# Turning blocks on all partitions at once, and copying them to their place, in a two-layer hybrid encoder

## The chip, the cores and the metric

The kernel runs on one core of a Trainium2 chip. The core has five engines, each with its own in-order stream of instructions: TensorE (PE in the profile) multiplies matrices, VectorE (DVE), ScalarE (ACT) and GpSimd (POOL) work elementwise, and SyncE (SP) here only issues transfers. The metric is the device time of one execution in microseconds (us), as the median over several runs. A profile is one further execution, recorded by the hardware.

## The reference

The input is one sequence of 256 positions with 2048 channels, in float32. There are two layers. Each layer is a token mixer with a residual, and then a gated MLP with a residual; a final normalisation follows.

```python
for i in range(DEPTH):                        # DEPTH = 2
    hn = rms_norm(h, mix_norm[i])
    h = h + (mixer_a if i % 2 == 0 else mixer_b)(hn, ...)
    h = h + conv_ffn(rms_norm(h, ffn_norm[i]), w_up[i], conv_w[i], conv_b[i], w_down[i])
return rms_norm(h, final_norm)

def conv_ffn(h, w_up, conv_w, conv_b, w_down):   # D_FF = 5632
    u = depthwise_conv3(h @ w_up) + conv_b       # along the positions
    gate, val = jnp.split(u, 2, axis=-1)
    return (jax.nn.silu(gate) * val) @ w_down
```

Mixer A (layer 0) is grouped-query attention: 16 query heads and 4 key/value heads of 128 channels, queries and keys normalised per head and rotated by their position. Mixer B (layer 1) has 24 heads of 128 channels in three groups of eight; the groups look at nearby positions at strides 1, 4 and 16, with a relative-position bias, and are weighted against each other by their softmax denominators. Both end in an output projection back to 2048 channels.

## The kernel before, in words

**Layout.** The 256 positions are held as 2 x 128: position 2p + m lies on partition p in half m. The residual stream `h` is a tile [128, 2, 2048]. A matrix product needs its left operand with channels on the partitions, so before each projection the activations have to be transposed: 16 tiles `xh` of 128 channels by 256 positions, called hT in the code.

**Projections.** Every product is computed to nearly full float32 precision from a high and a low half. `feed` (line 137) loads weights in pieces of 128 x 1024 on SP's queue into six raw buffers. `split_raw` (line 125) makes the halves: ScalarE copies the piece to the reduced type (`wh`, line 128), VectorE subtracts it from the original (`wl`, line 129). Three such pairs of buffers rotate. For each piece TensorE then runs 12 matmuls of 512 columns (lines 153 to 155: high x high, high x low, low x high, for two channel blocks and two halves of the positions). Such a piece with its 12 matmuls is called a unit here. `project` makes 512 output columns from eight units or more; `project2` makes two column blocks, holding back the part of the left operand that is ready last; `project_pair` (line 278 among its matmuls) does two column blocks of the MLP's down projection with one multiplication fewer per 2 x 2 block.

**Side work in steps.** Everything else, such as attention, the MLP's convolution and the transposes, is written as Python generators. `start` puts one in a list; after each unit, `step` (line 93) runs the first generator up to its next `yield`. So the number of yields says how many units later a piece of work is put into the program. The framework then orders each engine's instructions by its own estimate of when they are ready; the weight halves get a priority that lies 45 instructions ahead (`AHEAD`). At run time each engine works strictly through its own stream.

**Two ways to transpose without TensorE.** VectorE's transpose turns blocks of 32 x 32. To turn a whole tile, each block must also move from one group of 32 partitions to another.

- `block_T` (line 332, the instruction is on line 334) does both in one: it reads 32 partitions and writes 32 other ones. One call covers 32 x 256 elements, so 16 calls turn a tile [128, 2, 512].
- The MLP's convolution (`up_post`, lines 428 to 449) does it in two: two transposes of 128 x 512 turn the blocks where they lie (line 435), and then 16 copies of 32 x 256 put them on their partitions (lines 444, 446, 448). The string `PLACE = "pava"` says which engine copies to each of the four groups: GpSimd four of the 16, ScalarE eight, VectorE four.

`block_T` is used in two generators. `late_transpose` (line 337) turns 512 columns of `h` just after the residual was added, for the next projection, and is called for column blocks 0 to 2 at the end of both mixers (`out_proj`, line 661) and of the first MLP; block 3 goes over TensorE. Its last part, `put`, multiplies by the gain on ScalarE (line 294) and takes the low half on VectorE (line 297). `heads_T_dve` (line 699) turns four heads of keys or queries: mixer A's keys once, mixer B's keys and queries twelve times. In mixer B's groups 1 and 2 the result is used as it is (the low half is None); otherwise it is split into two halves (lines 290, 291). Mixer A's queries go over TensorE (`heads_T`).

**Order around it.** `add_residual` (line 388, VectorE) and `sumsq_cols` (line 329, two squares on ScalarE) run when a column block is done, then `late_transpose` follows over six steps: one to allocate its tile, four of four small transposes each, and one for the gains. In `project2` of mixer A the column blocks 0 and 1 are done two units apart, and blocks 2 and 3 eight units after one another, so that three transposes follow closely. Biases for mixer B are loaded on GpSimd's queue (line 928).

Of the kernel before, what the change touches and what calls it, by code (L numbers as in the profile page):

```python
# [13 lines left out]
P = 128  # L14
D = 2048
NT = 256
# [17 lines left out]
def tile_encoder(ctx: ExitStack, tc: tile.TileContext, x, xT, w_a, w_ao, q_gain, k_gain, w_b, w_bo,  # L34
# [294 lines left out]
            nc.scalar.activation(junk(), h[:, m, n * 512:(n + 1) * 512], AF.Square,  # L329
                                 accum_out=ss[:, m, n:n + 1])  # L330

    def block_T(o, s, b, g):
        rows, cols = slice(32 * g, 32 * g + 32), slice(32 * b, 32 * b + 32)
        nc.vector.transpose(o[cols].rearrange("p a (m t) -> p a m t", m=2)[:, :, :, rows],  # L334
                            s[rows].rearrange("p m (a c) -> p a m c", c=P)[:, :, :, cols])

    def late_transpose(hT, n, g, pool, tag):
        def put(kt, src):
            hT[kt] = new_hT(kt)
            split_scaled(*hT[kt][:2], src, gain[:, g, kt:kt + 1])  # L340

        yield
        if n < 3:
            t = pool.tile([P, 4, NT], F32, tag=tag, name=nm("tT"))
            for b in range(4):
                yield
                for gr in range(4):
                    block_T(t, h[:, :, n * 512:(n + 1) * 512], b, gr)
            yield
            for j in range(4):  # L350
                put(4 * n + j, t[:, j, :])
            return
        yield
        for kp in range(2):
            if kp:
                yield
            t = ps_tile()
            for j in range(2):
                kt = 4 * n + 2 * kp + j
                for m in range(2):  # L360
                    nc.tensor.transpose(t[:, j * NT + m * P:j * NT + (m + 1) * P],
                                        h[:, m, kt * P:(kt + 1) * P], ident)
            for j in range(2):
                put(4 * n + 2 * kp + j, t[:, j * NT:(j + 1) * NT])
# [31 lines left out]
    def ffn(l, hT, ss_in, g_next, last, side=None):  # L396
        with tc.tile_pool(name=nm("wpool"), bufs=1) as wp, tc.tile_pool(name=nm("fpool"), bufs=1) as fp:
# [29 lines left out]
            def up_post(acc, n, cs, after=None):  # L427
                u = us.pop(0)
                us.append(u)
                yield  # L430
                s = fp.tile([P, 2, 512], F32, tag="s", name=nm("s"))
                t = fp.tile([P, 2, 512], F32, tag="t", name=nm("t"))
                for m in range(2):
                    nc.scalar.activation(s[:, m], acc[m], AF.Copy, scale=rstd[:, m:m + 1])
                    nc.vector.transpose(t[:, m], s[:, m])  # L435
                yield
                tv = t.rearrange("p m (j q c) -> p j m q c", j=4, q=4)
                uv = u.rearrange("p j (m t) -> p j m t", m=2)
                for i in range(16):
                    a, b = i // 4, (i // 4 + i) % 4  # L440
                    dst = uv[32 * b:32 * b + 32, :, :, 32 * a:32 * a + 32]
                    src = tv[32 * a:32 * a + 32, :, :, b]
                    if PLACE[b] == "p":
                        nc.gpsimd.tensor_copy(dst, src)  # L444
                    elif PLACE[b] == "a":
                        nc.scalar.activation(dst, src, AF.Copy)  # L446
                    else:
                        nc.vector.tensor_copy(dst, src)
# [61 lines left out]
            for hf, (p0, p1) in enumerate(HALVES):  # L510
# [39 lines left out]
                def done(accs, n):  # L550
                    if hf == 1 and last:
                        for m in range(2):
                            cols = slice(n * 512, (n + 1) * 512)
                            hs = h[:, m, cols]
                            nc.vector.tensor_tensor(hs, accs[m], hs, ALU.add)
                            if n < 3:
                                nc.scalar.activation(junk(), hs, AF.Square, accum_out=ss[:, m, n:n + 1])
                                nc.gpsimd.tensor_tensor(hs, hs, fin[n], ALU.mult)
                            else:
                                nc.vector.scalar_tensor_tensor(junk(), hs, 1.0, hs, ALU.mult, ALU.mult,  # L560
                                                               accum_out=ss[:, m, n:n + 1])
                                finish(m)
                        if n == 2:
                            nc.vector.tensor_reduce(part, ss[:, :, :3], axis=AX.X, op=ALU.add)
                            nc.vector.tensor_scalar(part, part, 1.0 / D, EPS, op0=ALU.mult, op1=ALU.add)
                        return
                    add_residual(accs, n)
                    if hf == 1:
                        sumsq_cols(ss, n, junk)
                        start(late_transpose(hTn, n, g_next, fp, "tT"))  # L570

                def finish(m):
                    ms = small.tile([P, 1], F32, tag="ms", name=nm("ms"))
# [84 lines left out]
            assert not spare  # L658
        return hTn, ss

    def out_proj(w, slots, kgs, late, g_next, junk, pool, tag):
        hTn, ss = {}, new_ss()

        def done(accs, n):
            add_residual(accs, n)
            sumsq_cols(ss, n, junk)
            start(late_transpose(hTn, n, g_next, pool, tag))

        done(project2(w, 0, 1, slots, kgs, late, lambda a: done(a, 0)), 1)
        for n in (2, 3):  # L670
# [27 lines left out]

    def heads_T_dve(o, s, pool, tag):
        hi, lo = o  # L700
        t = hi if lo is None else pool.tile([P, 4, NT], F32, tag=tag, name=nm("tT"))
        for b in range(4):
            if b:
                yield
            for g in range(4):
                block_T(t, s, b, g)
        if lo is not None:
            split(hi, lo, t)

    def mixer_a():  # L710
        with tc.tile_pool(name="apool", bufs=1) as ap:
# [165 lines left out]

            for g in range(4):
                start(attend(g, project(w_a, g, hT, kgs)))
            return out_proj(w_ao, slots, kgs, 1, 1, junk, ap, "sq")  # L880

    scr0 = dpool.tile([8, P, 512], F32, name="scr0")
    scr1 = dpool.tile([16, P, 256], F32, name="scr1")
# [26 lines left out]
    def mixer_b(hT, ss_in):  # L910
        with tc.tile_pool(name="bpool", bufs=1) as bp:
# [26 lines left out]
            for hf in range(2):  # L938
# [102 lines left out]
            return out_proj(w_bo, slots, [0, 2, 4, 1, 3, 5], 3, 3, junk, bp, "vl")  # L1041

    hT, ss = mixer_a()
    hT, ss = ffn(0, hT, ss, 2, False, bias_lines)
# [86 lines left out]
```

## Time and profile before

| | |
|---|---|
| median of 3 runs | 2273.33 us (2270.11 to 2275.6) |
| the profiled execution | 2272.74 us |
| its span, first to last instruction | 2270.9 us |
| granted TensorE clock | 0.999 |
| DMA, mean over the span | 193 GB/s |

A line of the groups view names the line of the kernel, the engine, the operation, the tile written and those read, the shape and the count; then the busy time in us and the mean ns of one; then the engine's idle time just before these instructions and what ended most of it. A line of the timeline has the start and the duration in us, the engine, the line, the operation and the tiles, and in square brackets idle time just before it. A line of the list of waits has who waited, for whom, then the sum in us, the number of times and the longest. Matmuls overlap, and their ends are modelled.

### The profile page before, as it was taken

The page shows a single profiled execution, that of the slowest core. Times are in us where ns is not written, and L with a number is a line of the kernel's source. Part 1 is how long each engine was busy: PE and PEld are TensorE (multiplying, and loading weights), DVE is VectorE, ACT ScalarE, POOL GpSimd, SP SyncE. Part 2 cuts the span into 40 slices and gives each one's busy share as a digit, 9 for nine tenths or more (in the row PEclk, how much of TensorE's full clock was granted, in tenths as well). Part 3 has the DMA queues.
Part 4 walks back from the last instruction along what each step waited for, and adds up shares of the span by engine and source line. Part 5 has one row for each costly group of instructions (what it writes and reads, how often), then busy time and mean ns, then how long its engine had stood idle before and what let it go on. Part 6 is the DMA issues. An engine that isn't in the chain of part 4 may idle for free.

```text
span 2270.9 us, 28787 instructions
## 1 busy us (share of the span) xinstructions
PE 2251.8 (99%) x10169; PEld 1861.3 (82%) x10169; DVE 1758.8 (77%) x2521; ACT 1394.8 (61%) x2066; POOL 197.2 (9%) x284
## 2 busy tenths in 40 slices
PE   9999999999999999999999999999999999999998
PEld 7788788888888888888888888878888888888886
DVE  6877877878877778978876876586888788687784
ACT  6565477677547777545454454455777754577763
POOL 2210002210001010010000000000101100001110
PEclk9999999999999999999999999999999999999999
DMA  8444557755665665666555554555665656656653
GB/s 296 158 149 148 190 193 225 222 188 190 210 204 188 198 188 186 211 215 203 190 177 176 177 193 160 179 185 195 196 193 194 205 180 218 189 192 195 223 197 128
DMA packets 126449, 437.42 MB, mean 193 GB/s; under 512 B 17264, under 2 KB 18032, under 8 KB 126304
## 3 DMA queue, kind: packets, MB, share of 16 engines
q1 hardware_dynamic: 119744, 425.64, 57.2%
q0 software_dynamic: 6128, 9.38, 1.6%
q8 instruction: 79, 1.29, 0.2%
q10 hardware_dynamic: 432, 0.56, 0.1%
q14 instruction: 66, 0.54, 0.1%
HBM read 429.20 MB, written 6.29 MB: 192 GB/s over the span
## 4 chain that ended last, share of the span: by engine, by line
PE 81%; DVE 1%; DMA 1%; issue 0%; POOL 0%; ACT 0%; POOLq 0%; DVEq 0%; ACTq 0%
PE acc L154 21%; PE acc L153 21%; PE acc L155 21%; PE acc L273 5%; PE acc L275 5%; PE acc L278 5%; DMA scr<-lnt 1%; PE ps L305 1%; DVE wl L129 1%; PE ps L1009 0%; DVE tT L334 0%; PE ps L308 0%; PE ps L309 0%; PE ps L307 0%; DVE h L388 0%
## 5 line engine op out<-in xcount | busy, mean ns | idle before, releaser
L129 DVE TENSOR_TENSOR wl<-raw,wh 128x1024 fp32r<-128x1024 f32 x822 | 1007.1, 1229 | 354.9 <-ACT wh L128 350.2
L128 ACT ACTIVATE wh<-raw 128x1024 fp32r<-128x1024 f32 x822 | 867.0, 1058 | 622.0 <-PE acc L155 394.9
L153 PE MATMUL acc<-wh,xh 128*128 128x512 f32 x2176 | 852.0, 392 | 0.8 <-ACT wh L164 0.8
L154 PE MATMUL acc<-wl,xh 128*128 128x512 f32 x2176 | 848.6, 390 | 3.6 <-DVE wl L129 2.9
L155 PE MATMUL acc<-wh,xh 128*128 128x512 f32 x2176 | 847.6, 390 | 0.0
L154 PEld LDWEIGHTS acc<-wl,xh 128*128 128x128 f32 x2176 | 408.8, 188 | 89.9 <-DVE wl L129 6.4
L155 PEld LDWEIGHTS acc<-wh,xh 128*128 128x128 f32 x2176 | 408.5, 188 | 85.0
L153 PEld LDWEIGHTS acc<-wh,xh 128*128 128x128 f32 x2176 | 408.7, 188 | 84.8 <-ACT wh L164 1.6
L273 PE MATMUL acc<-wh,ah 128*128 128x512 f32 x524 | 204.1, 390 | 0.6 <-DVE h L388 0.6
L275 PE MATMUL acc<-wh,al 128*128 128x512 f32 x524 | 203.9, 389 | 0.0
L444 POOL COPY u<-t 32x256 f32<-32x256 f32 x176 | 110.7, 629 | 1039.9 <-DVE t L435 1031.7
L154 PE MATMUL acc<-wl,ah 128*128 128x512 f32 x480 | 187.9, 392 | 2.0 <-DVE wl L129 1.8
L153 PE MATMUL acc<-wh,ah 128*128 128x512 f32 x480 | 187.4, 390 | 0.0
L155 PE MATMUL acc<-wh,al 128*128 128x512 f32 x480 | 187.1, 390 | 0.0
L446 ACT ACTIVATE u<-t 32x256 f32<-32x256 f32 x352 | 147.8, 420 | 12.6 <-DVE t L435 4.6
L278 PE MATMUL acc<-wl,ah 128*128 128x512 f32 x524 | 146.0, 389 | 0.0
L273 PEld LDWEIGHTS acc<-wh,ah 128*128 128x128 f32 x524 | 98.4, 188 | 21.7 <-DVE h L388 1.3
L278 PEld LDWEIGHTS acc<-wl,ah 128*128 128x128 f32 x524 | 98.4, 188 | 20.5
L275 PEld LDWEIGHTS acc<-wh,al 128*128 128x128 f32 x524 | 98.3, 188 | 20.3
L154 PEld LDWEIGHTS acc<-wl,ah 128*128 128x128 f32 x480 | 90.1, 188 | 24.1 <-DVE wl L129 5.8
L155 PEld LDWEIGHTS acc<-wh,al 128*128 128x128 f32 x480 | 90.1, 188 | 18.4
L153 PEld LDWEIGHTS acc<-wh,ah 128*128 128x128 f32 x480 | 90.2, 188 | 18.3
(170 smaller groups left out, 1597.9 us busy)
## 6 DMA issues: line engine op xcount, KB each, us to landing
raw<-in_w_up_dram SPq DMA_DIRECT2D x352, 512.0 KB, 4.3
raw<-in_w_down_dram SPq DMA_DIRECT2D x176, 512.0 KB, 4.7
raw<-in_w_b_dram SPq DMA_DIRECT2D x144, 512.0 KB, 3.9
raw<-in_w_bo_dram SPq DMA_DIRECT2D x48, 512.0 KB, 3.9
raw<-in_w_a_dram SPq DMA_DIRECT2D x40, 512.0 KB, 4.4
raw<-in_w_ao_dram SPq DMA_DIRECT2D x32, 512.0 KB, 3.8
raw<-in_w_a_dram SPq DMA_DIRECT2D x16, 256.0 KB, 7.2
h<-in_x_dram SPq DMA_DIRECT2D x4, 512.0 KB, 7.6
```

The costliest lines, as they stand in the source:

```text
L128: nc.scalar.activation(wh, r, AF.Copy)
L129: nc.vector.tensor_tensor(wl, r, wh.bitcast(F32), ALU.subtract)
L153: nc.tensor.matmul(accs[m], xh, wh[:, j, :], start=st, stop=False)
L154: nc.tensor.matmul(accs[m], xh, wl[:, j, :], start=False, stop=False)
L155: nc.tensor.matmul(accs[m], xl, wh[:, j, :], start=False, stop=sp)
L273: nc.tensor.matmul(acc[k], xh, wh[:, j, :], start=k in fresh, stop=False)
L275: nc.tensor.matmul(acc[k], xl, wh[:, j, :], start=False, stop=False)
L278: nc.tensor.matmul(acc[k], xh, wl[:, j, :], start=False, stop=last[k] == i and j == 1)
L305: nc.tensor.matmul(o, lh[ls], rh[rs], start=start, stop=stop)
L444: nc.gpsimd.tensor_copy(dst, src)
L446: nc.scalar.activation(dst, src, AF.Copy)
```

## The change

Both generators now take the MLP's way. What stood in `up_post` becomes two helpers, `turn_blocks` and `place_blocks`, and `turned` joins them, with one `yield` between. Its string is `"paaa"`: four of the 16 copies go to GpSimd, twelve to ScalarE, none to VectorE. The MLP itself keeps `"pava"`.

`late_transpose` needs two tiles now, one for the turned blocks and one for the result, so it is given two tags; they name buffers that the pools already have (`sq` and `t2` in mixer A, `t` and `tT` in the MLP, `vl` and `kTh` in mixer B). Its gains are spread over two steps, two tiles each; the number of steps stays six. `heads_T_dve` writes the result straight into the target where there is no low half, and otherwise back over the staging tile, from which it is split; the number of steps stays the same here too.

```diff
-    def block_T(o, s, b, g):
-        rows, cols = slice(32 * g, 32 * g + 32), slice(32 * b, 32 * b + 32)
-        nc.vector.transpose(o[cols].rearrange("p a (m t) -> p a m t", m=2)[:, :, :, rows],
-                            s[rows].rearrange("p m (a c) -> p a m c", c=P)[:, :, :, cols])
+    def turn_blocks(s, pool, tag):
+        t = pool.tile([P, 2, 512], F32, tag=tag, name=nm("tT"))
+        for m in range(2):
+            nc.vector.transpose(t[:, m], s[:, m])
+        return t
+
+    def place_blocks(o, t, place):
+        tv = t.rearrange("p m (j q c) -> p j m q c", j=4, q=4)
+        for i in range(16):
+            a, b = i // 4, (i // 4 + i) % 4
+            dst = o[32 * b:32 * b + 32, :, :, 32 * a:32 * a + 32]
+            src = tv[32 * a:32 * a + 32, :, :, b]
+            if place[b] == "p":
+                nc.gpsimd.tensor_copy(dst, src)
+            elif place[b] == "a":
+                nc.scalar.activation(dst, src, AF.Copy)
+            else:
+                nc.vector.tensor_copy(dst, src)
+
+    def turned(o, s, pool, tag):
+        t = turn_blocks(s, pool, tag)
+        yield
+        place_blocks(o.rearrange("p j (m t) -> p j m t", m=2), t, "paaa")
...
         if n < 3:
-            t = pool.tile([P, 4, NT], F32, tag=tag, name=nm("tT"))
-            for b in range(4):
-                yield
-                for gr in range(4):
-                    block_T(t, h[:, :, n * 512:(n + 1) * 512], b, gr)
+            yield
+            o = pool.tile([P, 4, NT], F32, tag=tags[1], name=nm("tM"))
+            yield from turned(o, h[:, :, n * 512:(n + 1) * 512], pool, tags[0])
+            yield
             yield
             for j in range(4):
-                put(4 * n + j, t[:, j, :])
+                if j == 2:
+                    yield
+                put(4 * n + j, o[:, j, :])
             return
...
     def heads_T_dve(o, s, pool, tag):
         hi, lo = o
-        t = hi if lo is None else pool.tile([P, 4, NT], F32, tag=tag, name=nm("tT"))
-        for b in range(4):
-            if b:
-                yield
-            for g in range(4):
-                block_T(t, s, b, g)
+        dst = hi if lo is None else s.rearrange("p m c -> p (m c)").rearrange("p (j t) -> p j t", j=4)
+        yield from turned(dst, s, pool, tag)
+        yield
+        yield
         if lo is not None:
-            split(hi, lo, t)
+            split(hi, lo, dst)
```

More of the change, by code (lines that the diff above doesn't have):

```diff
@@ L330, in sumsq_cols, with late_transpose @@
                                  accum_out=ss[:, m, n:n + 1])
-    def block_T(o, s, b, g):
-        rows, cols = slice(32 * g, 32 * g + 32), slice(32 * b, 32 * b + 32)
-        nc.vector.transpose(o[cols].rearrange("p a (m t) -> p a m t", m=2)[:, :, :, rows],
-                            s[rows].rearrange("p m (a c) -> p a m c", c=P)[:, :, :, cols])
-    def late_transpose(hT, n, g, pool, tag):
+    def turn_blocks(s, pool, tag):
[19 more added lines that the diff above has]
+        place_blocks(o.rearrange("p j (m t) -> p j m t", m=2), t, "paaa")
+    def late_transpose(hT, n, g, pool, tags):
         def put(kt, src):
@@ L436, in up_post @@
                 yield
[L437 to L448, printed above, removed]
+                place_blocks(u.rearrange("p j (m t) -> p j m t", m=2), t, PLACE)
                 yield
@@ L569, in done @@
                         sumsq_cols(ss, n, junk)
-                        start(late_transpose(hTn, n, g_next, fp, "tT"))
+                        start(late_transpose(hTn, n, g_next, fp, ("t", "tT")))
                 def finish(m):
@@ L659, in ffn, with out_proj @@
         return hTn, ss
-    def out_proj(w, slots, kgs, late, g_next, junk, pool, tag):
+    def out_proj(w, slots, kgs, late, g_next, junk, pool, tags):
         hTn, ss = {}, new_ss()
@@ L666, in done @@
             sumsq_cols(ss, n, junk)
-            start(late_transpose(hTn, n, g_next, pool, tag))
+            start(late_transpose(hTn, n, g_next, pool, tags))
         done(project2(w, 0, 1, slots, kgs, late, lambda a: done(a, 0)), 1)
@@ L879, in mixer_a @@
                 start(attend(g, project(w_a, g, hT, kgs)))
-            return out_proj(w_ao, slots, kgs, 1, 1, junk, ap, "sq")
+            return out_proj(w_ao, slots, kgs, 1, 1, junk, ap, ("sq", "t2"))
     scr0 = dpool.tile([8, P, 512], F32, name="scr0")
@@ L1040, in mixer_b @@
                     start(v_gen(g, project(w_b, 6 * g + 4 + hf, hT, kgs)))
-            return out_proj(w_bo, slots, [0, 2, 4, 1, 3, 5], 3, 3, junk, bp, "vl")
+            return out_proj(w_bo, slots, [0, 2, 4, 1, 3, 5], 3, 3, junk, bp, ("vl", "kTh"))
     hT, ss = mixer_a()
```

## The prediction

> **What bounds the kernel now.** I read the head of the page first, then the same execution cut into stretches, then the list of who TensorE waited for, and last the timeline of one place where it waited.
>
> ```profile
> span 2270.9 us, 28787 instructions
> PE 2251.8 (99%) x10169; PEld 1861.3 (82%) x10169; DVE 1758.8 (77%) x2521; ACT 1394.8 (61%) x2066; POOL 197.2 (9%) x284
> PE acc L154 <- DVE wl L129: 4.7, 9, 1.0
> PE ps L309 <- DVE qTl L291: 0.8, 1, 0.8
> ```
>
> TensorE is busy for 99% of the span, so no other engine can win much: only what TensorE loses while waiting is for sale. Nearly all of it is one wait, matmul line 154 for `wl`, the low half of a split weight that VectorE makes. But the ends of matmuls are modelled, so a short gap is partly hidden inside "busy". The loss is better counted by starts. Here is one wait on TensorE, and VectorE's work ahead of it:
>
> ```profile
> 1491.41 0.39 PE L155 MATMUL acc<-wh,al 128*128 128x512 f32 x1
> 1491.64 0.39 PE L153 MATMUL acc<-wh,ah 128*128 128x512 f32 x1
> 1492.52 0.50 PE L154 MATMUL acc<-wl,ah 128*128 128x512 f32 x1 [0.49 <-DVE wl L129]
> 1492.85 0.40 PE L155 MATMUL acc<-wh,al 128*128 128x512 f32 x1
> ...
> 1485.46 2.23 DVE L334 STREAM_TRANSPOSE tT<-h 32x256 f32<-32x256 f32 x5
> 1487.72 1.23 DVE L129 TENSOR_TENSOR wl<-raw,wh 128x1024 fp32r<-128x1024 f32 x1
> 1488.97 2.23 DVE L334 STREAM_TRANSPOSE tT<-h 32x256 f32<-32x256 f32 x5
> 1491.24 1.22 DVE L129 TENSOR_TENSOR wl<-raw,wh 128x1024 fp32r<-128x1024 f32 x1
> ```
>
> An undisturbed matmul starts 0.227 us after the one before (1491.41 to 1491.64). This one started 0.88 us later, and the next 0.33 us after it: 0.76 us lost where the wait list books 0.49. The cause stands below: VectorE does five small transposes of line 334, then one `wl`, 3.5 us a round, while TensorE needs a new `wl` every 12 matmuls, 12 x 0.227 = 2.72 us. It falls 0.8 us back per round until the buffers are used up.
>
> Stretches (us; then TensorE, weight loads, VectorE, ScalarE, GpSimd, each with its instructions in brackets):
>
> ```profile
> 64.00:80.00 16.00, 14.95 (x63) 11.40 (x62) 14.04 (x22) 7.80 (x10) 2.08 (x2) 1.00 0.53 176
> 236.00:270.00 34.00, 32.79 (x139) 25.13 (x138) 32.16 (x55) 15.95 (x24) 0.00 (x0) 1.00 0.54 171
> 420.00:880.00 460.00, 460.00 (x2031) 380.84 (x2030) 372.37 (x501) 314.40 (x451) 38.73 (x60) 1.00 0.61 198
> 980.00:1370.00 390.00, 389.77 (x1821) 325.06 (x1820) 295.87 (x455) 198.66 (x298) 10.79 (x13) 1.00 0.59 190
> 1481.00:1500.00 19.00, 18.24 (x78) 14.08 (x77) 17.55 (x31) 9.65 (x16) 0.00 (x0) 1.00 0.52 168
> 1503.00:1533.00 30.00, 30.00 (x134) 24.83 (x133) 22.57 (x33) 14.39 (x19) 0.00 (x0) 1.00 0.59 194
> ```
>
> 1503 to 1533 is the yardstick: 30 us / 0.227 = 132.2 starts, and 134 matmuls touch the stretch, since a record of 0.39 us reaches over the borders. So starts are the count less 0.39 / 0.227 = 1.7. Then 64 to 80 (mixer A's keys) loses 16 - 61.3 x 0.227 = 2.1 us; 236 to 270 (output projection of mixer A) 34 - 137.3 x 0.227 = 2.8; 1481 to 1500 (output projection of mixer B) 19 - 76.3 x 0.227 = 1.7. Together 6.6 us, each good to one matmul. The same line 334 also runs in mixer B (980 to 1370), where TensorE was idle only 0.23 of 390 us: nothing is to be had from it there.
>
> **The change, part by part.**
>
> ```profile
> L334 DVE STREAM_TRANSPOSE tT<-h 32x256 f32<-32x256 f32 x144 | 62.8, 436 | 2.6
> L334 DVE STREAM_TRANSPOSE tT<-stg 32x256 f32<-32x256 f32 x64 | 27.9, 436 | 1.0
> L334 DVE STREAM_TRANSPOSE kT<-stg 32x256 f32<-32x256 f32 x64 | 27.9, 435 | 1.1
> L334 DVE STREAM_TRANSPOSE qT<-stg 32x256 f32<-32x256 f32 x64 | 27.9, 436 | 1.0
> L334 DVE STREAM_TRANSPOSE tT<-ro 32x256 f32<-32x256 f32 x16 | 7.0, 436 | 0.3
> L435 DVE STREAM_TRANSPOSE t<-s 128x512 f32<-128x512 f32 x88 | 62.1, 707 | 15.2 <-ACT s L434 15.2
> L446 ACT ACTIVATE u<-t 32x256 f32<-32x256 f32 x352 | 147.8, 420 | 12.6 <-DVE t L435 4.6
> L444 POOL COPY u<-t 32x256 f32<-32x256 f32 x176 | 110.7, 629 | 1039.9 <-DVE t L435 1031.7
> 219.00:268.00 49.00, 47.79 (x205) 37.59 (x204) 46.73 (x80) 25.47 (x41) 0.00 (x0) 1.00 0.53 172
> ```
>
> Removed: 352 transposes of 32x256, 16 for each of 22 turnings (9 of border activations, 12 of mixer B's keys and queries, 1 of mixer A's keys). Added, with prices from the MLP, whose convolution already works this way with the same shapes: per turning two 128x512 transposes (2 x 0.707 = 1.41 us of VectorE for 16 x 0.436 = 6.98), 12 copies on ScalarE (12 x 0.420 = 5.04 us) and 4 on GpSimd (4 x 0.629 = 2.5 us). Over the kernel VectorE loses 22 x 5.57 = 122 us, ScalarE gains 111, GpSimd 55. None of this is time by itself. What counts is the stretch. In 219 to 268, three turnings, VectorE is busy 46.73 of 49 us; without 48 x 0.436 and with 6 x 0.707 it is 30.0, or 61%. ScalarE goes from 25.47 to 25.47 + 36 x 0.420 = 40.6, or 83%. VectorE's backlog, which causes the 6.6 us, goes; ScalarE comes next, and how its copies lie between its weight copies decides.
>
> ```profile
> 1501.65 1.06 ACT L128 ACTIVATE wh<-raw 128x1024 fp32r<-128x1024 f32 x1 [1.04 <-PE acc L155]
> 1504.37 1.06 ACT L128 ACTIVATE wh<-raw 128x1024 fp32r<-128x1024 f32 x1 [1.66 <-PE acc L155]
> ...
> 1502.74 1.23 DVE L129 TENSOR_TENSOR wl<-raw,wh 128x1024 fp32r<-128x1024 f32 x1 [0.52 <-ACT wh L128]
> ...
> 709.50 1.06 ACT L128 ACTIVATE wh<-raw 128x1024 fp32r<-128x1024 f32 x1 [1.08 <-PE acc L155]
> 710.59 2.64 ACT L446 ACTIVATE u<-t 32x256 f32<-32x256 f32 x6
> 713.26 1.06 ACT L128 ACTIVATE wh<-raw 128x1024 fp32r<-128x1024 f32 x1
> 714.34 0.85 ACT L446 ACTIVATE u<-t 32x256 f32<-32x256 f32 x2
> ```
>
> The margin: TensorE's end of one unit of 12 matmuls frees a buffer, `wh` starts at 1501.65, `wl` ends at 1502.74 + 1.23 = 1503.97. Of three buffers two are ahead, so TensorE wants it two units and one matmul later, at 1501.65 + 5.44 + 0.23 = 1507.32. A pair may be 3.35 us late before it costs anything. ScalarE has 1.66 us free per unit. The MLP shows how its copies fall: six (2.64 us), a `wh` that is 713.26 - 709.50 - 2.72 = 1.04 us late, then the rest; and from 420 to 880, full of such bursts, TensorE has no gap. Twelve copies in two such gaps make the second `wh` about 2 us late, inside the margin. If all twelve ran in one gap, it would be 5.04 - 1.66 = 3.38 us: on the edge. So I cost the copies at nothing where they run alone, the cover being the third buffer, and at one small stall (0.76 us, the one shown) in two places where other ScalarE work falls in with them: 1.5 us. The bounds are 0 and the 33 us of the second rival.
>
> By the Trainium skill, page "ScalarE: Activation LUTs", section "What ACT_TABLE_LOAD costs", a copy without pointer operands takes 186 ns + 0.833 ns per element: an estimate of 399 ns here, 4.79 us for twelve, where the row has 420. By it a burst in one gap would come 3.13 us late and inside the margin; the sum goes by the row.
>
> GpSimd's four copies end well inside ScalarE's 5.04 us. In mixer B its queue also issues the bias loads; they move behind at most four copies (2.5 us) and are read only after the query projection, so nothing waits. No load is added or moved. SP's weight loads wait for a free raw buffer, freed when `wh` and `wl` are made: up to 2 us later in a burst, under the same margin with six raw buffers. Each copy adds a wait for the two transposes; behind it on ScalarE stand `wh` and the gain copies. ScalarE waits there today:
>
> ```profile
> 1496.05 0.51 ACT L294 ACTIVATE xh<-tT,gain 128x256 fp32r<-128x256 f32 x1 [5.89 <-DVE tT L334]
> L329 ACT ACTIVATE junk<-h 128x512 f32<-128x512 f32 x32 | 20.1, 628 | 5.7 <-DVE h L388 4.0 <-DMA h<-in_x_dram 0.7
> 710.94 1.35 DVE L129 TENSOR_TENSOR wl<-raw,wh 128x1024 fp32r<-128x1024 f32 x1
> ```
>
> 5.89 us in which no `wh` is made because the gain copy ahead of it waits for line 334; with 1.41 us of transposes this wait shrinks. The added yields keep the count of steps (border: six, heads: as before), so results are due at the same unit. Queries and keys with a low half now keep their staging tile until the split, two units longer; its next writer comes 8 units on at the earliest. Nothing for either.
>
> Sum: 6.6 recovered, 1.5 given back, -5.1 us. The profiled execution took 2272.74 us (span 2270.9 and 1.8 around it): 2267.6. The median of the runs, 2273.33, lies 0.6 above it, so the forecast is 2273.3 - 5.1 = 2268.2 us.
>
> **The rivals.** First, ScalarE takes VectorE's place. For it: 83% in 219 to 268, and waits of others in the same in-order queue. Then mixer A's projection keeps its 2.8 us and the two small stalls stay: -6.6 + 2.8 + 1.5 = -2.3, 2271.0 us. Against it: the MLP's gapless 460 us at 314.40 busy, 68%.
>
> Second, the slower side: bursts overrun the margin. If twelve copies sit in one gap with other ScalarE work, such as the two squares of the residual (2 x 0.628 = 1.26 us) or a split, `wh` is about 4.7 us late and TensorE loses some 1.4, with the restart 1.5. In all 22 turnings 33 us; it decides from 6.6 / 1.5, about five, on. With half of them: 11 x 1.5 - 6.6 = +9.9, 2283.2 us. Against it: the burst of the MLP is broken by `wh` after six.
>
> Third, GpSimd and VectorE collide. With a copy beside it `wl` takes 1.35 for 1.23 us, so a collision costs 0.12. Were VectorE held for all of each copy, 4 x 0.629 = 2.5 us per turning would come off the 5.57 it saves, the net staying positive: if that leaves half the stalls, -3.3 + 1.5 = -1.8, 2271.5 us. The page "SBUF — State Buffer" of the Trainium skill, section "Who interferes with whom", states such a lock: a VectorE operation with two SBUF inputs and a GpSimd instruction that reads SBUF exclude each other for a whole instruction. By that rule this rival; the row bears out only the short hold.
>
> Fourth, more is gained: the query wait (0.8) goes too and no stall is new: -7.4, 2265.9 us.
>
> **How the numbers follow.** About 0.2% (4.5 us) is what a measurement of this kernel can tell from no change: faster is below 2268.8, slower above 2277.9. Forecast 0.45, first rival 0.22, second 0.18, third 0.05, fourth 0.10. The forecast lies so near the border that a quarter of it falls to "same". Faster: 0.75 x 0.45 + 0.10 = 0.44. Slower: 0.18. Same: the rest, 0.38. The range goes from 2264.8, the fourth less 1 us of scatter, into the second rival to 2280, above which some 0.12 lie. Of faster and same alone it would be 2265 to 2273.
>
> **What would show it.** Right: line 334 gone, TensorE's wait for `wl` down from 4.7 to under 2 us, counts at one per 0.227 us in the three stretches, ScalarE near 1506 busy, copies in runs of six or fewer, VectorE near 1636. Wrong: runs of twelve copies with a late `wh` behind them and waits of TensorE in mixer B, where there are none today.

## The result and the profile after

The changed kernel takes 2266.97 us (median of 20 runs, 2264.64 to 2275.98), the kernel before, measured beside it, 2272.99 us (20 runs, 2270.11 to 2277.48). The ratio is 0.9977, with a 95% interval of 0.9971 to 0.9984. By the ratio that is 5.2 us less, between 3.6 and 6.6; the two medians lie 6.0 us apart. The profiled execution took 2266.05 us, with a span of 2264.2.

First the head of the page of the changed kernel, engine by engine.

```profile
span 2264.2 us, 28877 instructions
PE 2248.7 (99%) x10169; PEld 1861.7 (82%) x10169; DVE 1635.8 (72%) x2213; ACT 1504.0 (66%) x2330; POOL 252.8 (11%) x372
```

VectorE is 123 us less busy than before, ScalarE 109 more, GpSimd 56 more. TensorE, which sets the time, does the same work and is busy for 99% of the span as it was. 123 us less work on one engine moved the end by some 5 us.

The groups of the changed kernel for the border activations show the new work (the engine, the tile written from the tile read, the count, busy us, mean ns):

```profile
L335 DVE STREAM_TRANSPOSE tT<-h 128x512 f32<-128x512 f32 x18 | 12.4, 700 | 2.4 <-ACT tM L347 2.4
...
L347 ACT ACTIVATE tM<-tT 32x256 f32<-32x256 f32 x108 | 44.8, 415 | 2.7 <-DVE xh L297 0.7 <-DVE tT L335 0.5
...
L345 POOL COPY tM<-tT 32x256 f32<-32x256 f32 x36 | 23.0, 638 | 308.9 <-DVE tT L335 288.3 <-DVE xh L297 19.4
```

All three prices, 0.700, 0.415 and 0.638 us, lie within 1.5% of those that the prediction took from the MLP (0.707, 0.420, 0.629).

The list of waits of the changed kernel, TensorE's (sum in us, times, longest):

```profile
PE acc L154 <- DVE wl L129: 1.9, 4, 0.8
...
PE acc L154 <- DVE wl L165: 1.1, 1, 1.1
PE ps L309 <- DVE qTl L291: 0.6, 1, 0.6
```

The wait for `wl` fell from 4.7 us in nine places to 1.9 in four. The stretches that the prediction counted, cut again from the changed kernel (columns as there: TensorE, weight loads, VectorE, ScalarE, GpSimd, granted clock, DMA):

```profile
64.00:80.00 16.00, 15.40 (x67) 12.12 (x66) 9.33 (x8) 14.08 (x22) 4.96 (x7) 1.00 0.60 203
236.00:270.00 34.00, 33.48 (x148) 27.33 (x147) 22.47 (x29) 27.30 (x48) 3.01 (x5) 1.00 0.61 199
980.00:1370.00 390.00, 389.77 (x1826) 325.08 (x1825) 230.79 (x296) 258.06 (x444) 41.31 (x61) 1.00 0.59 188
1481.00:1500.00 19.00, 19.00 (x86) 15.73 (x85) 9.97 (x12) 13.24 (x22) 1.67 (x3) 1.00 0.61 194
```

Counted in the prediction's way (the count less 1.7, times 0.227 us): the keys of mixer A lose 16 - 65.3 x 0.227 = 1.2 us where they lost 2.1; its output projection 34 - 146.3 x 0.227 = 0.8 for 2.8; the output projection of mixer B nothing for 1.7. Of 6.6 us, 2.0 are left: 4.6 gained. In mixer B itself (980 to 1370) VectorE is 65 us less busy, ScalarE 59 more, and TensorE exactly as busy as before, 389.77 us: twelve of the 22 turnings changed nothing.

The output projection of mixer B shows how it was won. This is ScalarE in the timeline of the changed kernel, where before the gain copies waited 5.89 us behind line 334:

```profile
1479.29 1.07 ACT L128 ACTIVATE wh<-raw 128x1024 fp32r<-128x1024 f32 x1 [0.29 <-PE acc L155]
1480.38 2.55 ACT L347 ACTIVATE tM<-tT 32x256 f32<-32x256 f32 x6
1482.95 1.06 ACT L128 ACTIVATE wh<-raw 128x1024 fp32r<-128x1024 f32 x1
1484.04 2.54 ACT L347 ACTIVATE tM<-tT 32x256 f32<-32x256 f32 x6
1486.61 1.06 ACT L128 ACTIVATE wh<-raw 128x1024 fp32r<-128x1024 f32 x1
1487.58 1.69 ACT L294 ACTIVATE xh<-tM,gain 128x256 fp32r<-128x256 f32 x4
1489.18 2.06 ACT L128 ACTIVATE wh<-raw 128x1024 fp32r<-128x1024 f32 x2
```

The weight copy at 1479.29 starts as soon as TensorE frees its buffer. Six copies follow, a weight copy that comes 1482.95 - 1479.29 - 2.72 = 0.94 us late, six more copies, and a weight copy another 0.94 us later, 1.9 us in all; then the gain copies without a wait and two weight copies in a row, and ScalarE is level again. These are the two bursts of six and the second `wh` "about 2 us late" of the prediction, and TensorE loses nothing.

The keys of mixer A are the place that did not come clean. ScalarE, VectorE and TensorE there, from the timeline of the changed kernel:

```profile
57.68 1.06 ACT L128 ACTIVATE wh<-raw 128x1024 fp32r<-128x1024 f32 x1 [2.13 <-PE acc L155]
62.54 0.84 ACT L347 ACTIVATE ro<-tT 32x256 f32<-32x256 f32 x2 [3.80 <-DVE tT L335]
63.41 1.06 ACT L128 ACTIVATE wh<-raw 128x1024 fp32r<-128x1024 f32 x1
64.50 3.40 ACT L347 ACTIVATE ro<-tT 32x256 f32<-32x256 f32 x8
67.92 1.06 ACT L128 ACTIVATE wh<-raw 128x1024 fp32r<-128x1024 f32 x1
...
69.01 1.23 DVE L129 TENSOR_TENSOR wl<-raw,wh 128x1024 fp32r<-128x1024 f32 x1 [3.20 <-ACT wh L128]
...
69.44 0.39 PE L153 MATMUL acc<-wh,xh 128*128 128x512 f32 x1
70.29 0.50 PE L154 MATMUL acc<-wl,xh 128*128 128x512 f32 x1 [0.47 <-DVE wl L129]
```

The first two copies stand ahead of a weight copy in ScalarE's stream and wait 3.80 us for the transposes; eight more follow after only one weight copy. Then VectorE waits 3.20 us for ScalarE's `wh`, where before ScalarE and TensorE had waited for VectorE (ScalarE's split of the keys 5.42 us for line 334). TensorE wanted that `wl` at 69.67 and started at 70.29. Two things had made ScalarE late by then, its wait and the number of its copies. The runs below change the number; the one meant to take the wait away left it in place.

### The profile page after: what moved, and what is told of

Same layout as the page of the kernel before. It is cut to its first block, busy times and chain, and to the rows that moved or that the text cites. A ratio compares the mean times of both kernels' runs of the same rounds, so it can differ in the third digit from the quotient of the medians.

```text
span 2264.2 us, 28877 instructions
## 1 busy us (share of the span) xinstructions
PE 2248.7 (99%) x10169; PEld 1861.7 (82%) x10169; DVE 1635.8 (72%) x2213; ACT 1504.0 (66%) x2330; POOL 252.8 (11%) x372
## 4 chain that ended last, share of the span: by engine, by line
PE 96%; ACT 1%; DVE 1%; issue 1%; DMA 1%; POOL 0%; SPq 0%; POOLq 0%; DVEq 0%; ACTq 0%
PE acc L154 26%; PE acc L155 26%; PE acc L153 26%; PE acc L273 5%; PE acc L275 5%; PE acc L278 5%; PE ps L305 1%; PE ps L309 1%; PE ps L308 1%; PE ps L307 0%; DVE wl L129 0%; PE ps L868 0%; ACT tM L347 0%; ACT wh L128 0%; PE ps L1016 0%
```

## The experiments

All edits are to the changed kernel unless it is said otherwise. The ratio is always to the kernel before, timed beside it. Since all the profiles run the same matmuls, I also followed the gain through the program: the start of each weight copy on ScalarE against the same-numbered one in the profile of before (us, minus is earlier than before; the head of the columns is its time before). "+lnt" names an edit that comes further down.

```
                 53     95    273    368    429    674   1312   1591   2251
changed       -0.95  -1.85  -4.03  -3.39  -4.50  -4.49  -4.44  -6.05  -6.37
borders only  -1.06  -1.05  -3.31  -2.87  -4.54  -3.71  -3.73  -5.40  -5.38
heads only    -0.98  -1.89  -1.95  -1.46  +0.95  +1.43  +1.43  +1.51  +1.16
bursts of 12  -1.11  +0.04  -0.55  -0.03  +0.45  +0.43  +5.49  +6.44  +7.08
GpSimd 8      -1.01  -3.09  -5.92  -5.83  -2.18  -1.73  -1.67  -3.27  -3.61
GpSimd 8 +lnt -1.04  -3.15  -5.99  -5.94  -8.07  -6.13  -6.08  -7.73  -8.49
```

Most of the first column is no gain of the change: every profile in the table, that of "bursts of 12" too, is about 1 us ahead of before's by then, and the kernel before with nothing but the bias lines spaced out (below), the same program up to there, is 0.56 ahead. TensorE waited longer at the head of that one execution. In the changed kernel mixer A's keys give 0.9 us (95), its output projection 2.2 (273), mixer B's output projection 1.6 (1591), and mixer B nothing (-4.49 to -4.44 from 674 to 1312). The 0.6 us lost between 273 and 368 are lost by the kernel before with its bias lines spaced out too (0.6), and by the versions with eight copies on GpSimd they are not; this differs from one profile to the next and was not followed up. The 1.1 us between 368 and 429 are another thing, told below.

**Border activations alone.** Keys and queries as before (`block_T` comes back as it was; this is left out of the two diffs that use it).

```diff
 def heads_T_dve(o, s, pool, tag):
     hi, lo = o
-    dst = hi if lo is None else s.rearrange(...)
-    yield from turned(dst, s, pool, tag)
-    yield
-    yield
+    t = hi if lo is None else pool.tile([P, 4, NT], F32, tag=tag, name=nm("tT"))
+    for b in range(4):
+        if b:
+            yield
+        for g in range(4):
+            block_T(t, s, b, g)
     if lo is not None:
-        split(hi, lo, dst)
+        split(hi, lo, t)
```

> Only the border activations take the new way; keys and queries keep the small transposes. Theory (the gain is what TensorE waited for wl in three stretches, and nothing else): of the 6.0 us gained by the whole change the output projections give 2.2 less 0.7 in mixer A and 1.7 in mixer B, so 3 to 4.5 us below the kernel before, about 2269. Rival (the gain follows the VectorE time saved, wherever it is): 9 of 22 turnings, 2.5 us below, about 2270.5. A further rival: the 1.1 us won near 399 us, in the first MLP, are a matter of chance in when a transfer lands; then that part is there or not without regard to the edit.

2267.30 us (6 runs) beside 2274.08: 0.9973 (0.9962 to 0.9984). Two of its stretches:

```profile
64.00:80.00 16.00, 14.99 (x64) 11.48 (x63) 14.07 (x20) 8.76 (x11) 3.14 (x2) 1.00 0.53 171
236.00:270.00 34.00, 33.49 (x148) 27.39 (x147) 22.47 (x29) 27.33 (x50) 2.92 (x6) 1.00 0.62 199
```

The keys lose 16 - 62.3 x 0.227 = 1.9 us, as before; the output projection 0.8, as with the whole change. Nine turnings of the 22 carry nearly all of the gain; within the intervals the time cannot be told from that of the whole change.

**Keys and queries alone.** The reverse: `late_transpose` with `block_T` and one tag.

```diff
-            yield
-            o = pool.tile([P, 4, NT], F32, tag=tags[1], name=nm("tM"))
-            yield from turned(o, h[:, :, n * 512:(n + 1) * 512], pool, tags[0])
-            yield
+            t = pool.tile([P, 4, NT], F32, tag=tags[0], name=nm("tT"))
+            for b in range(4):
+                yield
+                for gr in range(4):
+                    block_T(t, h[:, :, n * 512:(n + 1) * 512], b, gr)
```

> Only keys and queries take the new way; the border activations keep the small transposes. Theory: mixer A's keys give 0.7 to 0.9 us, mixer B's twelve turnings nothing, since TensorE was idle 0.23 us there: 0.5 to 1.5 us below the kernel before, about 2272, with the waits at 240 to 270 and 1490 to 1500 us back. Rival (saved VectorE time counts): 13 of 22 turnings, 3.5 us below, 2269.5.

2272.64 us (12 runs) beside 2274.08: 0.9988 (0.9978 to 0.9998). Its stretches:

```profile
236.00:270.00 34.00, 32.79 (x138) 25.17 (x137) 32.22 (x53) 16.61 (x25) 0.00 (x0) 1.00 0.55 173
980.00:1370.00 390.00, 389.76 (x1820) 325.02 (x1819) 229.85 (x289) 258.48 (x443) 41.30 (x61) 1.00 0.60 190
1481.00:1500.00 19.00, 18.51 (x80) 14.31 (x78) 17.55 (x29) 9.64 (x16) 0.00 (x0) 1.00 0.53 176
```

Both output projections lose again about what they lost before (34 - 136.3 x 0.227 = 3.1 and 19 - 78.3 x 0.227 = 1.2 us, for 2.8 and 1.7), with VectorE at 95% and 92%; mixer B is as full as ever. Of this half only the keys of mixer A count, 0.9 us; the lead stands still at +1.43 all through mixer B. (The 2.4 us lost before 429 are the bias lines, below.)

**All twelve copies in one gap.** The same copies, with a priority that lets the framework place them before the next weight copy. This forces the prediction's second rival.

```diff
-        place_blocks(o.rearrange("p j (m t) -> p j m t", m=2), t, "paaa")
+        with tc.high_priority(offset=200):
+            place_blocks(o.rearrange("p j (m t) -> p j m t", m=2), t, "paaa")
```

> The changed kernel, with the copies put ahead of the weight copies, so that ScalarE runs all twelve of a turning in one go. Theory (margin of 3.35 us; a burst makes the next wh 5.04 - 1.66 = 3.38 us late): nothing in the turnings where ScalarE has no other work, some 1.4 to 1.5 us in those where squares, a split or gains fall in: between 6 and 12 of 22, so +9 to +18 us on the changed kernel, 2276 to 2285. Rival (the margin is wider in truth, ScalarE never matters): 2267. Rival (every burst stalls): 22 x 1.5 = 33, about 2300.

2277.86 us (11 runs) beside 2274.08: 1.0015 (1.0005 to 1.0025), slower than before, and 0.4% slower than the change itself. All 22 turnings now run as twelve. My expectation that a lone burst is free failed. One in mixer B, from its timeline:

```profile
1083.48 1.06 ACT L128 ACTIVATE wh<-raw 128x1024 fp32r<-128x1024 f32 x1 [1.08 <-PE acc L155]
1084.57 5.11 ACT L347 ACTIVATE qT<-tT 32x256 f32<-32x256 f32 x12
1089.70 3.00 ACT L128 ACTIVATE wh<-raw 128x1024 fp32r<-128x1024 f32 x3
...
1090.79 3.50 DVE L129 TENSOR_TENSOR wl<-raw,wh 128x1024 fp32r<-128x1024 f32 x3 [4.99 <-ACT wh L128]
...
1091.44 0.39 PE L153 MATMUL acc<-wh,xh 128*128 128x512 f32 x1
1092.07 0.50 PE L154 MATMUL acc<-wl,xh 128*128 128x512 f32 x1 [0.24 <-DVE wl L129]
1092.41 0.40 PE L155 MATMUL acc<-wh,xh 128*128 128x512 f32 x1
```

`wh` is 1089.70 - 1083.48 - 2.72 = 3.50 us late. TensorE starts 0.63 and then 0.34 us after the matmul before, 0.40 and 0.11 more than 0.227: 0.51 us. So a pair may come 3.50 - 0.40 = 3.1 us late, not 3.35. The same step of 0.63 us stands at seven more of mixer B's twelve bursts, and one of 0.92 at a ninth; in the table 5.06 us are lost from 674 to 1312. In the MLP's down projection, which keeps four pairs, three bursts of twelve, one of them at 932 us, cost nothing. That would fit a deeper buffer; but the units there are of another kind, so the fourth pair is not shown to be the reason.

**Eight copies to GpSimd.** If the number of copies on ScalarE holds up the keys, fewer must help, and if GpSimd disturbs VectorE, more of its copies must hurt.

```diff
-        place_blocks(o.rearrange("p j (m t) -> p j m t", m=2), t, "paaa")
+        place_blocks(o.rearrange("p j (m t) -> p j m t", m=2), t, "ppaa")
```

> The changed kernel with eight copies on GpSimd and eight on ScalarE per turning, for four and twelve. Theory (ScalarE is what is late now, in mixer A's keys and at 241 us): eight copies are 3.36 us, the stall at 241 us (0.8) goes and about half of the 1.1 us in the keys: 1 us below the changed kernel, about 2266. Rival (GpSimd and VectorE exclude each other): VectorE is held for up to 0.4 us by each of eight copies, wl comes late and the time is 1 to 3 us above the changed kernel, 2268 to 2270, with wl's mean up from 1233 ns.

2265.49 us (7 runs) beside 2274.08: 0.9966 (0.9954 to 0.9978). The two stretches in which something was left:

```profile
64.00:80.00 16.00, 16.00 (x72) 13.28 (x71) 10.57 (x9) 12.30 (x18) 7.71 (x11) 1.00 0.68 220
236.00:270.00 34.00, 34.00 (x152) 27.86 (x151) 23.68 (x29) 22.15 (x37) 6.47 (x10) 1.00 0.64 200
```

Both are full: 16 - 70.3 x 0.227 = 0.0 and 34 - 150.3 x 0.227 = -0.1 us lost. Up to 368 its lead is -5.83 against the change's -3.39. ScalarE was what remained in the way; GpSimd's copies do VectorE no harm that TensorE feels. `wl` takes 1.234 us in the mean, 1.233 in the changed kernel and 1.229 before. (Its lead then falls by 3.65 us between 368 and 429, for the bias lines again; the profiled execution took 2268.81 us, 3.3 above its median.)

**The same with four copies on VectorE instead.**

```diff
-        place_blocks(o.rearrange("p j (m t) -> p j m t", m=2), t, "paaa")
+        place_blocks(o.rearrange("p j (m t) -> p j m t", m=2), t, PLACE)
```

`PLACE` is the MLP's `"pava"`: GpSimd four, ScalarE eight, VectorE four.

> The changed kernel with the MLP's own split of the copies: four on GpSimd, eight on ScalarE, four on VectorE. Theory (ScalarE's number of copies is what is late): the stalls in mixer A's keys and at 241 us shrink as with eight on GpSimd, since VectorE has 3 us of idle time there; 1.5 to 2.5 us below the changed kernel. Rival (VectorE is still the tighter engine in the projections): waits for wl come back between 236 and 270 us and the time is that of the changed kernel or above.

2264.51 us (6 runs) beside 2273.63: 0.9960 (0.9946 to 0.9974). Both stretches are full here too. The two agree within their intervals: it matters that ScalarE has eight copies, and who has the other four makes no difference that these runs can tell.

**A longer way between turning and placing the keys.** If instead the wait of 3.80 us ahead of the weight copy holds up the keys, placing the copies a unit later must take it away.

```diff
-    def turned(o, s, pool, tag):
+    def turned(o, s, pool, tag, gap=1):
         t = turn_blocks(s, pool, tag)
-        yield
+        for _ in range(gap):
+            yield
...
-                yield from heads_T_dve(kT, ro, ap, "sq")
+                yield from heads_T_dve(kT, ro, ap, "sq", 2)      # one yield less behind it
```

> The changed kernel, with mixer A's keys placed one unit later after the turning (two yields between, one fewer behind; the split stays at its step). Theory (ScalarE sits idle 3.8 us at 58.7 to 62.5 because a copy stands ahead of wh in its queue and waits for a late transpose): that wait goes or shrinks below 1 us, the two stalls of 0.74 and 0.40 us at 69 to 74 go, 1 us below the changed kernel, about 0.997 of the kernel before. Rival (ScalarE is late by the number of copies, not by the wait): the stalls stay, since still twelve copies come in three units; no change. Rival: keys get late and TensorE waits longer for the first scores at 88 us.

2267.18 us (12 runs) beside 2273.63: 0.9973 (0.9963 to 0.9983), no different from the change. Its ScalarE:

```profile
62.99 0.84 ACT L347 ACTIVATE ro<-tT 32x256 f32<-32x256 f32 x2 [3.80 <-DVE tT L335]
```

The wait did not go. A `yield` says when work enters the program; where it stands in ScalarE's stream is the framework's estimate, and that put the two copies in the same place. TensorE's stalls there came to lie elsewhere, with about the same sum. So this edit does not test the wait. With eight copies the same wait of 3.80 us stands in the profiles of both versions above, and the keys lose nothing: the wait with eight copies fits into the margin, the wait with twelve does not. Twelve copies without the wait were not tried in the keys.

**The bias lines.** The timelines also showed a loss that the change does not touch. While the first MLP runs, the lines of mixer B's bias table go out over one buffer of two halves, `lnt`, in six steps; VectorE's copy into it (line 911) waits until the transfer of two steps ago has left. VectorE's waits for this, first of the changed kernel, then of the one with eight copies on GpSimd (sum, times, longest):

```profile
DVE lnt L911 <- DMA scr<-lnt: 3.3, 2, 2.2
```

```profile
DVE lnt L911 <- DMA scr<-lnt: 7.8, 2, 4.6
```

Behind that copy in VectorE's stream stands `wl`. TensorE lost 1.3 us there in the profile of before and 0.2 in that of the change, which is the 1.1 of the table; against that 1.3 the profiles with +0.95 and -2.18 in the column of 429 us lost 3.7 and 5.0. The edit spaces the steps out:

```diff
             for b in range(6):
-                for _ in range(2):
+                for _ in range(6):
                     yield
```

> The changed kernel, with six units instead of two between the bias lines of the first MLP, so that a line buffer is written again only long after the transfer out of it was issued. Theory (the 0 to 5 us lost near 396 us, different in each profile, are VectorE waiting for such a transfer with wl behind it): VectorE's waits for scr, 3.3 us in the changed kernel and 7.8 us in the one with eight copies on GpSimd, go to zero, the stall at 396 us with them; the median falls by 1 to 2 us and the runs lie closer together. Rival (the loss there comes from elsewhere, or the wait moves to another line): no change in the median.

> Eight copies on GpSimd and eight on ScalarE, and six units between the bias lines. Theory (both losses are separate): 2.4 us below the changed kernel by the copies, where the profile before the bias lines stood 5.8 against 3.4 us ahead, and 1 to 2 us more by the lines: about 10 us below the kernel before, ratio 0.9955. Rival (GpSimd's transfers of the bias lines are held back by the copies): the waits for scr come back.

> The kernel before, with nothing changed but six units for two between the bias lines. Theory (the wait for those transfers belongs to both kernels and is chance): its waits for scr, 4.7 us in the kernel before, go; the median falls by 1 to 2 us to about 2272 and the runs lie closer together, so that the change itself, free of this chance, is worth the difference to the changed kernel with the same edit, 4 to 6 us. Rival (the wait is longer in the kernel before because VectorE is loaded more, and part of the change's gain): its median falls by more, and the two kernels with the edit lie less than 4 us apart.

> Copies four, eight and four on GpSimd, ScalarE and VectorE, and six units between the bias lines. Theory (the gain of both edits adds, and the copies are as good on VectorE as on GpSimd): within 1 us of the kernel with eight on GpSimd and the same lines, about 2263, ratio 0.995 to 0.9965. Rival (VectorE's stalls come back): 2 us above that.

The change with it: 2266.06 us (6 runs, 2265.10 to 2267.82), 0.9966 (0.9954 to 0.9978). The kernel before with it: 2272.30 (11 runs), 0.9994 (0.9985 to 1.0003), no gain that can be told. Against the change without it, 0.9977, the intervals overlap. No profile with the spacing shows the wait any more, but all four have a loss of 1.0 to 1.7 us in the MLP's down projection, at about 600 us. Two profiles without the spacing have it as well (keys and queries as before, and `"pava"`), so the spacing is not shown to be its cause. (In the table the spacing also moves bias matmuls from ahead of 429 us to behind it, so that of the -8.07 only what stands at 674 is gained.) With the edit on both sides the change is worth 0.9966 / 0.9994 = 0.9972, the same as without as far as the intervals tell: the bias lines are not shown to be any part of its gain.

With eight copies on GpSimd and the spacing the kernel takes 2263.63 us (6 runs, 2262.38 to 2265.14), 0.9954 (0.9942 to 0.9966), the fastest here; with `"pava"` and the spacing 2263.88 (5 runs), 0.9959 (0.9947 to 0.9972). TensorE's waits in the former:

```profile
PE acc L154 <- DVE wl L129: 0.9, 2, 0.8
PE acc L154 <- DVE wl L165: 0.9, 1, 0.9
PE ps L309 <- DVE qTl L291: 0.6, 1, 0.6
```

The three stretches are full in these two versions. Of the 0.9 us for `wl`, 0.8 are a stall at 60 us, ahead of the keys, which stands in the kernel before as well.

## Why the prediction was right, step by step

**The bound, and where there was something to win: right.** Three stretches by name, counted by starts, and nothing elsewhere. The two halves of the change show the three places one by one, and the twelve turnings in mixer B gave nothing. The forecast of -5.1 us stands against -5.2 (3.6 to 6.6). That it is so close is in part luck: the three places give 4.6 by the count, and the interval is 3 us wide.

**The prices of the parts: right.** VectorE -123 us for -122, ScalarE +109 for +111, GpSimd +56 for +55. In 219 to 268 VectorE came out at 66% for the 61% of the prediction, ScalarE at 85% for 83%.

**What is given back: the size was right, the cause was named in one of two places.** I took 1.5 us for two small stalls where "other ScalarE work falls in with" the copies. 2.0 us remained by the count, so that one of the three stretches came out full where the prediction had asked for three: 0.8 at 241 us and 1.2 in the keys. At 241 us two bursts of six follow close behind the gain copies of the turning before, so other ScalarE work did fall in with them; the same two bursts alone, at 1480 us, cost nothing. At the larger of the two stalls in the keys (0.74 us) it was no other ScalarE work, but the copies' own wait together with their number; only ahead of the smaller one (0.40 us, at 73.4) stands the split. I had written that the wait behind the transposes "shrinks". At the output projection of mixer B it did (5.89 us to none). At the keys it shrank only from 5.42 us to 3.80, because the copies now wait where the split had waited, and a weight copy stands behind them. Eight copies instead of twelve clear both places.

**The margin of 3.35 us: 3.1 measured.** The sum used it only to say that twelve in one gap are "on the edge". They are over it, by 0.4 us. Of the missing 0.25 us, 0.05 is the way from the end of `wl` to the matmul (1089.70 to 1092.07 is 2.37 us, and I had 2.32). The other 0.20 is a slip in the prediction, and stands in the profile of before at the place that it used: it counted the 5.44 + 0.23 us from the start of `wh` at 1501.65, but they run from the first matmul of the unit that TensorE was then starting, 0.20 us earlier. TensorE wanted that `wl` at 1507.12, not at 1507.32:

```profile
1501.45 0.39 PE L153 MATMUL acc<-wh,ah 128*128 128x512 f32 x1
1507.12 0.39 PE L154 MATMUL acc<-wl,ah 128*128 128x512 f32 x1
```

 "Runs of six or fewer" held for nearly all: the changed kernel has 32 runs of six, and one each of seven, eight and twelve.

**The rivals.** The first, ScalarE in VectorE's place, is what is left of the stalls, but under a third of the size I gave it in the output projection (0.8 us for 2.8). The second, overrun bursts, is real when forced: the slower side came, at 0.5 us for a lone burst where I had said 1.5 with other work beside it. In the change it stayed away: the framework put a weight copy after six nearly everywhere. The third, GpSimd against VectorE, is refuted in its price: with twice the copies on GpSimd the stretches are full, and with the bias lines spaced out on both sides that version took 2263.63 us where the change, timed beside it, took 2266.06. With it falls, for this kernel, the price that I derived from the lock in the Trainium skill, page "SBUF — State Buffer", section "Who interferes with whom". The lock itself does show, in the starts and ends of the changed kernel's trace. All 66 GpSimd copies that start while a `wl` runs end 0.25 to 0.27 us after that `wl`; the others take 0.39 us in the middle. The other way round, a `wl` that starts during a copy takes 1.35 us in the middle for 1.22, and never over 1.45: VectorE waits at most for what is left of the one copy that is running. So the 0.629 us at which the prediction took a copy were already a mean of copies that had waited and copies that had not. Over the kernel the mean of `wl` moved by 0.005 us. One group of GpSimd's copies in the changed kernel (shortest, middle and longest ns):

```profile
L345 POOL COPY qT<-tT x16: 387/394/1426, 1077.8 to 1338.7; 32x256 f32<-32x256 f32 x16
```

The longest takes 1.03 us more than the middle one, nearly a `wl` of 1.23. Most of the waiting is GpSimd's, and no wait of TensorE in the changed kernel's list is for GpSimd.

The fourth rival had the query wait go; it went from 0.8 to 0.6 us.

**What the profile could not say.** Its span fell by 6.7 us, more than the medians. Of that 0.6 to 1 us is the head of before's execution and about 1 the bias lines, both different from one execution to the next. Two single profiles would have given too large a gain.

## What to carry to other kernels

Where one engine is busy 99%, count the starts of its instructions in each stretch; what they fall short by is all that a change beside it can win. Time freed where they fall short by nothing was worth nothing here. Work moved into another engine's in-order stream must fit between the deadlines there: find the margin (here 3.1 us with three buffer pairs) and set the longest burst, and any wait that stands ahead of it, against that. If a little is left, move a few instructions off the engine that is late before touching anything else; here GpSimd and VectorE could both take them.

## What the runs showed of the hardware that I had not expected

A stall of TensorE can cost more than its length. After the bias-line stall in the profile with eight copies on GpSimd, matmuls start every 0.43 us instead of 0.227, and the granted clock is halved. Its timeline, then that stretch (the third number from the end is the granted clock, which is back at 1.00 behind 401.6):

```profile
393.62 0.39 PE L153 MATMUL acc<-wh,xh 128*128 128x512 f32 x1
397.15 0.50 PE L154 MATMUL acc<-wl,xh 128*128 128x512 f32 x1 [3.15 <-DVE wl L129]
...
398.44 0.63 PE L155 MATMUL acc<-wh,xh 128*128 128x512 f32 x1
398.87 0.63 PE L153 MATMUL acc<-wh,xh 128*128 128x512 f32 x1
```

```profile
398.00:401.60 3.60, 3.60 (x11) 2.83 (x10) 2.36 (x2) 2.06 (x3) 0.60 (x1) 0.54 0.78 211
```

So 3.3 us of waiting cost 5 us. The same slow stretch of about 3.4 us follows a gap of 2.31 us between two starts in the profile with the keys and queries alone (granted clock 0.56 from 401.4 to 405), and two gaps of 1.37 and 1.26 us in a row in that with bursts of twelve (0.60 from 72 to 76). No other profile has it between its first 20 us and its last matmul, and there no two starts lie more than some 1.8 us apart. The Trainium skill, page "TensorE: Matmul & The Clock Gate", section "Part 1: The HAM clock gate", gives the half clock to a TensorE that was idle for a whole free-running window of about 3.4 us. The length of the slow stretch agrees; the condition does not, since here gaps of 2.3 us, and two of 1.3, were enough.

The traces say a little more. In each of the three the clock falls a whole number of 3.413 us (115, 116 and 19 of them) after it first rose in that execution. The 3.413 us that end there, with eight copies on GpSimd, with keys and queries alone and with bursts of twelve (the second number is TensorE's busy time):

```profile
394.49:397.91 3.42, 0.76 (x3) 0.66 (x4) 2.35 (x4) 0.38 (x1) 2.04 (x4) 1.00 0.21 56
397.77:401.19 3.42, 1.50 (x7) 0.93 (x6) 2.35 (x4) 0.53 (x1) 2.19 (x4) 1.00 0.28 76
68.37:71.78 3.41, 1.67 (x6) 0.86 (x5) 2.04 (x2) 3.38 (x5) 0.00 (x0) 1.00 0.01 2
```

They hold 2.66, 1.92 and 1.74 us without a matmul. Cut into pieces in the same way, the twelve profiles have no other piece, up to the last full one before the last matmul, with more than 1.39 us. A limit at about half a piece would fit; no run was made to test it.

The scatter of the times would fit such slow stretches (the change ran from 2264.6 to 2276.0 us, with the bias lines spaced out from 2265.1 to 2267.8). The granted clock on record for each execution points the same way: the run of 2276.0 us has 0.997, the other 19 of the changed kernel 0.998 or 0.999. But only the profiled executions have a trace, so that remains argued.
